# Counting split units anew in each stage of a hybrid decoder block

## The chip, the cores and the metric

The kernel runs on one core of a Trainium2 chip. The metric is the device time of one execution in microseconds (us), given as the median of several runs. An execution can also be recorded by the hardware profiler; the profile then shows the work of each engine: TensorE (PE, with its weight loads as PEld), VectorE (DVE), ScalarE (ACT), GpSimd (POOL) and SyncE (SP), which issues most of the DMA transfers here.

## The reference

One layer of a decoder block on 256 tokens of width 2048, in float32:

```
x = x + 0.5 * ffn1(rms_norm(x))                 # SwiGLU, hidden width 5632
z = rms_norm(x) @ w_in                          # 2048 -> 5120, five parts of 1024
y_lru = rg_lru(conv4(z0)) * gelu(z1)            # recurrent half
y_sc  = z2 * conv3(z3 * z4)                     # short convolution half
x = x + concat(rms_norm(y_lru), rms_norm(y_sc)) @ w_out
x = x + 0.5 * ffn2(rms_norm(x))
out = rms_norm(x)

ffn(h) = (silu(h @ w_gate) * (h @ w_up)) @ w_down
```

All matrix products are asked for in float32. The profile shows 339.82 MB read from HBM, nearly all of it weights, each used once for 256 rows.

## The kernel before

**Units and split parts.** Weights are worked off in *units* of 512 x 512 values, a tile of 128 x 2048 float32 (1 MB). `load` (L181) fetches a unit into one of three buffers of the pool `raws`. TensorE multiplies in a reduced float32 form, so each unit is split into two tiles of that form: `hi`, a rounded copy made by ScalarE in two halves, and `lo`, what is left (`raw - hi`), made by VectorE (`parts_of`, L210, and `low_part`, L204). A usual unit then takes 24 matmuls (the column products of the mixer are arranged otherwise): for each of two 128-row halves of the tokens, eight with `hi` and four with `lo`. In parts of the work seven products instead of eight are formed from a 2 x 2 arrangement of units (`seven`, L413); there a unit that belongs to the seven products takes 12 matmuls, and VectorE also forms sums and differences of raw units. Of those, two raw units are held longer and have buffers of their own (tag `kept`).

**Split buffers.** `split_tiles` (L194) hands out the pair of tiles for `hi` and `lo`. The pool `splits` lives for the whole kernel and has two such pairs, used in turn. While the list `extra` holds a pool, every third unit goes to that pool instead, in which there is one pair (where `extra[0]` is `bigs`, the pair comes from that general pool, which also lives for the whole kernel). `turn_of["split"]` counts the units; it is raised only while `extra` is not empty, and it is never set back.

**Stages.** They follow each other in this order. The first feed-forward part, `ffn(1, ...)` (L523), opens the pool `ffn1` and puts it into `extra`. The mixer opens two pools for the small tiles of the recurrent and the convolution halves; its column products take their split tiles from `splits` alone, and only `sc_c` (L1141) puts `bigs` into `extra`, for one call of `seven`. Still inside the mixer, the first quarter of the columns of `w_out` is multiplied (units named `o0_...`), with `extra` empty. Then the pool `outs` (L1253) is opened and put into `extra`: the last quarter of the columns (`o3_...`, four units) and a call of `seven` for the two middle ones (`o_q`, eleven units). Then `ffn(2, ...)` opens its pool `ffn2`. The pools of the mixer, of `outs` and of `ffn2` are opened one after the other on the same stack of memory, so a tile in a later pool can lie where tiles of the earlier one were, and its first writer waits until the earlier pool is out of use.

**Names in the profile.** Tiles are named after what they belong to, with numbers left out: `hi_g` and `hi_u` are the first units of gate and up weights of a feed-forward part, `hi_o` those of `o0` and `o3`, `hi_o_q_p` and `hi_o_q_x` those of `o_q` (`p` for the seven products, `x` for the others). In `outs`, `own` (L1294) and `done` (L1290) add results to the residual `xres` by VectorE; the last of these adds reads a saved product, `s_o_q`, which lies in the pool `outs`.

**The start of the second feed-forward part.** Its loop (L771) takes units in the order gate 0, up 0, gate 1, up 1, gate 2, up 2, gate 3, up 3, each with `unit` and `joint`, and between them calls the functions listed in `follow` (L633): the transposes of the residual's second quarter, the norm factor `r` and its row of factors (`pb`, `bc`), then the scaled and transposed quarters 2 and 3 (`xn`, `pt`, `units`), which are the other operand of gate 2, up 2, gate 3 and up 3. Of the adds into the residual, those for its third quarter come last.

**Order.** SyncE's transfers, TensorE's opening and the whole of the first feed-forward part's opening are held in the order of the program text. Elsewhere the framework plans the order of the instructions on each engine, from program order and from what its plan takes to be ready; on the chip each engine then works in that order, with semaphore waits that the framework sets.

Of the kernel before, what the change touches and what calls it, by code (L numbers as in the profile page):

```python
# [49 lines left out]
def hybrid_block(ctx: ExitStack, tc: tile.TileContext, a: dict, out: bass.AP):  # L50
# [13 lines left out]
    def flush():  # L64
        while pending:
            pending.popleft()[1]()
# [12 lines left out]
    bigs = ctx.enter_context(tc.tile_pool(name="bigs", bufs=10, side="left"))  # L79
# [5 lines left out]
    def bank(name):  # L85
        return psum.tile([P, 512], F32, tag="ps", name=name)
# [85 lines left out]
    def big(name):  # L172

        return bigs.tile([P, UK, 2 * S], F32R, tag="big", name=name)
# [2 lines left out]

    extra = []
    turn_of = {"split": 0}

    def load(src, name, pieces=((0, UK),), loaded=None, kept=False):  # L181
        if kept and extra[0] is not bigs:
            raw = extra[0].tile([P, UK, CW], F32, tag="kept", name=f"raw_{name}", bufs=2)
        elif kept:
            raw = bigs.tile([P, UK, CW], F32, tag="big", name=f"raw_{name}")
        else:
            raw = raws.tile([P, UK, CW], F32, tag="raw", name=f"raw_{name}")
        for i, e in pieces:
            sp.dma_start(raw[:, i:e, :], src[i * P : e * P].rearrange("(j p) c -> p j c", p=P))
            if loaded:  # L190
                loaded(i)
        return raw
# [185 lines left out]
    def seven_of(sf, x0, x1, v, spare, parts, meanwhile=None):  # L378

        a11, a12, a21, a22 = v[0, 0], v[0, 1], v[1, 0], v[1, 1]
        parts = dict(zip((4, 5, 6, 2), parts))
        quads = {4: spare, 5: a11, 6: a21, 2: a12}
        sf.update({0: stationary(x0, 0), 1: stationary(x1, 0), 3: stationary(x1, 1)})

        def high(i):
            hi, lo = parts[i]
            act.copy(hi, quads[i])
            sf[i] = [(hi[:, j, :], lo[:, j, :]) for j in range(UK)]  # L390

        def low(i):
            hi, lo = parts[i]
            dve.tensor_tensor(lo, quads[i], f32(hi), op=ALU.subtract)

        def two():
            dve.tensor_tensor(a21, a11, a21, op=ALU.subtract)
            dve.tensor_tensor(a11, spare, a11, op=ALU.subtract)

        def last():  # L400
            dve.tensor_tensor(a12, a12, a11, op=ALU.subtract)

        dve.tensor_tensor(spare, a21, a22, op=ALU.add)
        high(4)
        if meanwhile:
            meanwhile()
        low(4)
        return two, last, high, low

    def quad(tile):  # L410
        return tile.rearrange("p (j c) -> p j c", j=UK)
# [110 lines left out]

    def ffn(tag, norm, after, opening=False):  # L523
        with tc.tile_pool(name=f"ffn{tag}", bufs=1, side="left") as fp:
            extra.append(fp)
            wg, wu, wd = (a[f"ffn{tag}_w_{s}"][0] for s in ("gate", "up", "down"))

            def keep(name, dt=F32):
# [426 lines left out]
    def to_mixer(c, t):  # L955
# [4 lines left out]
        else:  # L960
            held["nm"].later(c)

    ffn(1, n1, to_mixer, True)
    nm = held["nm"]

# [3 lines left out]
    with tc.tile_pool(name="mixer", bufs=1, side="left") as mp, tc.tile_pool(name="mixw", bufs=2, side="left") as mw:  # L969
# [15 lines left out]
        def tmp(tag, name, w=S, dt=F32, bufs=2):  # L985
            return mw.tile([P, w], dt, tag=tag, name=f"{tag}_{name}", bufs=bufs)
# [154 lines left out]
        def sc_c(between):  # L1141
            r2 = work.tile([P, NT], F32, tag="r2", name="r2")
            dve.tensor_tensor(r2, nm.r, nm.r, op=ALU.mult)
            rt = [r2[:, t : t + 1] for t in range(NT)]
            room = [tmp(tag, "snap", 4 * S, bufs=1) for tag in "vd"]
            free = [b[:, o : o + CW] for b in room for o in (0, CW)]
            z = {}

            def turn(n):
                for f in range(0, 4, 2):  # L1150
                    pt = bank(f"pt_c{n}_{f}")
                    for i in range(2):
                        for t in range(NT):
                            o = i * S + t * P
                            pe.transpose(pt[:, o : o + P], z[t, n][:, (f + i) * P : (f + i + 1) * P], ident)
                    for i in range(2):
                        q = 4 * (1 - n) + f + i
                        c = tmp("cc", q, S + 2, bufs=8)
                        nc.gpsimd.memset(c[:, :2], 0.0)
                        act.copy(c[:, 2:], pt[:, i * S : (i + 1) * S])  # L1160
                        cc[q] = c

            def done(t, n, ps, tiles):
                for p in tiles[1:]:
                    dve.tensor_tensor(tiles[0], tiles[0], p, op=ALU.add)
                    free.append(p)
                if tiles:
                    z[t, n] = tiles[0]
                    dve.scalar_tensor_tensor(z[t, n], ps, rt[t], z[t, n], op0=ALU.mult, op1=ALU.add)
                else:  # L1170
                    z[t, n] = free.pop()
                    act.activation(z[t, n], ps, AF.Copy, scale=rt[t])
                if (t, n) == (1, 0):
                    turn(1)

            c0 = 3 * (D // 2)
            extra.append(bigs)
            seven(
                w_in, (0, 1), (c0 + CW, c0), si, [(u, nm.xT[u]) for u in (2, 3)], "in_c", lambda name: free.pop(0), done,
                lambda i: between() if i == 1 else None,  # L1180
                factor={"s1": rt[0], "s5": rt[1], "u2": rt[0], "u3": rt[1]},
            )
            extra.clear()
            return lambda: turn(0)
# [27 lines left out]
        for i, (use, part, half) in enumerate(order):  # L1212
            ps = columns(w_in, part * (D // 2) + half * CW, nm.xT, f"in_{part}_{half}", behind)
            behind = None
            if i == 0:
                flush()
                nm.factor()
                nm.diagonals()
                nm.rows()
                bc = nm.bc  # L1220
                behind = sc_c(lambda: use(ps, half))
                gate_weights("a", a["lru_w_a"][0])
                gate_weights("i", a["lru_w_i"][0])
                yT += [big(f"yT_{u}") for u in range(KD // UK)]
            else:
                use(ps, half)
# [6 lines left out]
        def add(c, t, g, *parts):  # L1233
            xr = xres[:, t, c * CW : (c + 1) * CW]
            for p in parts:
                dve.scalar_tensor_tensor(xr, p, rs[g][:, t : t + 1], xr, op0=ALU.mult, op1=ALU.add)
# [14 lines left out]


    with tc.tile_pool(name="outs", bufs=1, side="left") as op:  # L1253
        extra.append(op)

        def snapshot(name):
            return op.tile([P, CW], F32, tag="snap", name=name, bufs=4)

        so = {}
        pair = [big(f"ys_{i}") for i in range(2)]  # L1260
        halves_of = [(b[:, :, o : o + P], b[:, :, o + P : o + S]) for b in pair for o in (0, S)]
        quads = {(t, u): yv[0][:, :, u * S + t * P : u * S + (t + 1) * P] for t in range(NT) for u in range(2)}
        spare = quad(op.tile([P, CW], F32, name="yspare"))
        two, last_sum, high, low = seven_of(so, yT[0], yT[1], quads, spare, halves_of)

        def part(i):
            high(i)
            low(i)

        steps = {  # L1270
            (0, 0): [two, lambda: part(5)], (0, 1): [lambda: part(6)],
            (1, 0): [last_sum, lambda: part(2)], (1, 1): [],
        }
        for g in range(2):
            ps = product(
                w_out, 3, (2 * g, 2 * g + 1), yT.__getitem__, f"o3_{g}",
                between=lambda i: [fn() for fn in steps[g, i]],
            )
            for t in range(NT):
                add(3, t, g, ps[t])  # L1280
        n2.later(3, False)
        flush()
        left = {1: 4, 2: 4}

        def added(c):
            left[c] -= 1
            if not left[c]:
                n2.later(c, c < 2)

        def done(t, n, ps, tiles):  # L1290
            add(2 - n, t, 0, *([] if ps is None else [ps]), *tiles)
            added(2 - n)

        def own(t, n, ps):  # L1294
            add(2 - n, t, 1, ps)
            added(2 - n)

        seven(
            w_out, (0, 1), (2 * CW, CW), so, [(u, yT[u]) for u in (2, 3)], "o_q", snapshot, done, own=own
        )  # L1300
        extra.clear()
# [34 lines left out]
    def close(t, y3, h, n):  # L1336
# [24 lines left out]
        for engine, begin, end in ((dve, 0, 256), (dve, 256, 896), (act, 896, 1536), (dve, 1536, 2048)):  # L1361
# [6 lines left out]
            nc.sync.dma_start(ov[:, t, o], xo)  # L1368

    ffn(2, n2, last)  # L1370


# [28 lines left out]
```

## Time and profile before

| | |
|---|---|
| median of 3 runs | 1736.88 us (1736.38 to 1737.58) |
| profiled execution, its own time | 1733.94 us |
| its span, first to last instruction | 1732.2 us |
| PE busy | 1716.9 us (99%) |
| PEld busy | 1434.8 us (83%) |
| DVE busy | 1510.4 us (87%) |
| ACT busy | 1076.7 us (62%) |
| moved by DMA | 343.22 MB, mean 198 GB/s |
| mean granted TensorE clock | 0.997 |

Times in the profile are microseconds from the first instruction. The span is shorter than the execution's own time by what lies before the first and after the last instruction, and the profiled execution need not be the median one. "Idle" before an instruction is the time for which its engine did nothing, and the name behind the arrow is what ended it. A busy PE is not one at its peak, since matmuls are pipelined and their ends are modelled; an idle PE is idle.

### The profile page before, as it was taken

What the parts mean: (1) busy time and instruction counts of PE and PEld (TensorE: products, weight loads), DVE (VectorE), ACT (ScalarE), POOL (GpSimd) and SP (SyncE); (2) the same over time, 40 slices, a digit from 0 to 9 for tenths busy, and PEclk for the clock granted to TensorE, in tenths of its full rate; (3) what the DMA queues carried; (4) which work ended last, traced back from release to release, by engine and by line L of the source; (5) the groups of instructions that cost most, each with busy time, mean ns of one, the idle gap of its engine ahead of it and who ended that gap; (6) DMA issues with size and microseconds to landing.
All of it is one profiled execution on the core that took longest, in us unless ns stands there. A gap on an engine that the chain in (4) does not pass through costs nothing.

```text
span 1732.2 us, 20321 instructions
## 1 busy us (share of the span) xinstructions
PE 1716.9 (99%) x7985; PEld 1434.8 (83%) x7985; DVE 1510.4 (87%) x1239; ACT 1076.7 (62%) x1406; POOL 7.0 (0%) x34
## 2 busy tenths in 40 slices
PE   9999999999999999999999989999999999999998
PEld 8888888888888888888888878888888888888886
DVE  7998999899789887887897878889899887899895
ACT  7766566656566666666866556666556664556664
POOL 0100000000000000000000000000000000000000
PEclk9999999999999999999999999999999999999999
DMA  8564665666465646555566463575665646555743
GB/s 300 191 244 143 209 228 189 201 217 229 164 215 196 210 172 216 179 180 185 170 195 218 171 233 132 194 243 191 200 210 188 228 149 219 194 195 194 252 161 122
DMA packets 174223, 343.22 MB, mean 198 GB/s; under 512 B 5684, under 2 KB 8624, under 8 KB 174000
## 3 DMA queue, kind: packets, MB, share of 16 engines
q1 hardware_dynamic: 173632, 340.81, 58.1%
q8 instruction: 62, 1.02, 0.2%
q10 hardware_dynamic: 176, 1.06, 0.1%
q14 instruction: 33, 0.27, 0.0%
q0 software_dynamic: 320, 0.07, 0.0%
HBM read 339.82 MB, written 2.10 MB: 197 GB/s over the span
## 4 chain that ended last, share of the span: by engine, by line
PE 99%; DVE 0%; ACT 0%; issue 0%; DVEq 0%; ACTq 0%
PE ps_d L43 14%; PE ps_in L43 10%; PE ps_g_a L43 9%; PE ps_u_a L43 9%; PE ps_u_c L43 6%; PE ps_g_c L43 6%; PE ps_d_a L43 5%; PE ps_u_d L43 5%; PE ps_g_d L43 5%; PE ps_d_c L43 3%; PE ps_u_e L43 3%; PE ps_g_e L43 3%; PE ps_g L43 3%; PE ps_o L43 3%; PE ps_u L43 3%; PE ps_d_d L43 3%
## 5 line engine op out<-in xcount | busy, mean ns | idle before, releaser
L43 ACT CAST hi_g_p<-raw_g 128x1024 fp32r<-128x1024 f32 (+1 forms) x139 | 142.1, 1056 | 110.5 <-DVE raw_g L43 39.0
L43 DVE TENSOR_TENSOR lo_g_p<-raw_g,hi_g_p 128x2048 fp32r<-128x2048 f32 x70 | 159.6, 2287 | 32.8 <-ACT hi_g_p L43 32.7
L43 ACT CAST hi_u_p<-raw_u 128x1024 fp32r<-128x1024 f32 x140 | 141.4, 1050 | 66.2 <-PE ps_u_a L43 26.7
L43 DVE TENSOR_TENSOR lo_u_p<-raw_u,hi_u_p 128x2048 fp32r<-128x2048 f32 x70 | 159.2, 2287 | 15.1 <-ACT hi_u_p L43 14.8
L43 PE MATMUL ps_d<-hi_d,h 128*128 128x512 f32 x696 | 166.1, 390 | 0.0
L43 PEld LDWEIGHTS ps_d<-hi_d,h 128*128 128x128 f32 x696 | 130.0, 188 | 26.6
L43 ACT CAST hi_d<-raw_d 128x1024 fp32r<-128x1024 f32 x88 | 88.5, 1048 | 67.7 <-PE ps_u_d L43 19.9
L43 DVE TENSOR_TENSOR lo_d<-raw_d,hi_d 128x2048 fp32r<-128x2048 f32 x44 | 100.7, 2290 | 33.4 <-ACT hi_d L43 33.4
L43 PE MATMUL ps_in<-xT_nm,hi_in 128*128 128x512 f32 x512 | 122.5, 391 | 0.0
L43 ACT CAST hi_d_p<-raw_d 128x1024 fp32r<-128x1024 f32 x84 | 85.1, 1049 | 57.5 <-DVE raw_d L43 34.9
L43 PEld LDWEIGHTS ps_in<-xT_nm,hi_in 128*128 128x128 f32 x512 | 94.1, 188 | 18.9 <-ACT tha L43 0.5
L43 ACT CAST hi_u_x<-raw_u 128x1024 fp32r<-128x1024 f32 x80 | 80.6, 1047 | 38.7 <-PE ps_u_c L43 23.9
L43 ACT CAST hi_g_x<-raw_g 128x1024 fp32r<-128x1024 f32 (+1 forms) x79 | 81.3, 1059 | 32.4 <-PE ps_g_c L43 22.6
L43 DVE TENSOR_TENSOR raw_u<-raw_u,raw_u 128x2048 f32<-128x2048 f32 x40 | 91.6, 2290 | 10.7 <-DMA raw_u<-in_ffn_w_up_dram 10.0
L43 DVE TENSOR_TENSOR lo_d_p<-raw_d,hi_d_p 128x2048 fp32r<-128x2048 f32 x42 | 95.6, 2287 | 5.0 <-ACT hi_d_p L43 4.9
L43 DVE TENSOR_TENSOR lo_g_x<-raw_g,hi_g_x 128x2048 fp32r<-128x2048 f32 x40 | 91.5, 2287 | 8.4 <-ACT hi_g_x L43 8.4
L43 DVE TENSOR_TENSOR lo_in<-raw_in,hi_in 128x2048 fp32r<-128x2048 f32 x32 | 73.3, 2289 | 26.3 <-ACT hi_in L43 25.9
L43 DVE TENSOR_TENSOR raw_g<-raw_g,raw_g 128x2048 f32<-128x2048 f32 x40 | 91.5, 2288 | 5.0 <-DMA raw_g<-in_ffn_w_gate_dram 4.5
L43 DVE TENSOR_TENSOR lo_u_x<-raw_u,hi_u_x 128x2048 fp32r<-128x2048 f32 x40 | 91.4, 2286 | 0.8 <-ACT hi_u_x L43 0.4
L43 PE MATMUL ps_d<-lo_d,h 128*128 128x512 f32 x348 | 86.2, 389 | 0.0
L43 ACT CAST hi_in<-raw_in 128x1024 fp32r<-128x1024 f32 x64 | 64.0, 1046 | 24.9 <-PE ps_in L43 15.3
L43 PEld LDWEIGHTS ps_d<-lo_d,h 128*128 128x128 f32 x348 | 65.3, 188 | 13.6
(471 smaller groups left out, 3741.2 us busy)
## 6 DMA issues: line engine op xcount, KB each, us to landing
raw_d<-in_ffn_w_down_dram SPq DMA_DIRECT2D x88, 1024.0 KB, 5.2
raw_u<-in_ffn_w_up_dram SPq DMA_DIRECT2D x87, 1024.0 KB, 5.2
raw_g<-in_ffn_w_gate_dram SPq DMA_DIRECT2D x86, 1024.0 KB, 5.3
raw_in<-in_w_in_dram SPq DMA_DIRECT2D x32, 1024.0 KB, 5.1
raw_in_c<-in_w_in_dram SPq DMA_DIRECT2D x8, 1024.0 KB, 5.3
raw_o<-in_w_out_dram SPq DMA_DIRECT2D x8, 1024.0 KB, 5.1
raw_o_q<-in_w_out_dram SPq DMA_DIRECT2D x8, 1024.0 KB, 5.2
xres<-in_x_dram SPq DMA_DIRECT2D x3, 512.0 KB, 9.5
```

What stands on the lines that cost most here:

```text
L43: ins = getattr(self.engine, name)(*args, **kwargs)
```

## The change

A helper `more_from` puts a pool into `extra` and sets the count of split units back to zero. The three places that put a pool into `extra` call it.

```diff
     extra = []
     turn_of = {"split": 0}
+
+    def more_from(pool):
+        extra.append(pool)
+        turn_of["split"] = 0
...
     def ffn(tag, norm, after, opening=False):
         with tc.tile_pool(name=f"ffn{tag}", bufs=1, side="left") as fp:
-            extra.append(fp)
+            more_from(fp)
...
             c0 = 3 * (D // 2)
-            extra.append(bigs)
+            more_from(bigs)
             seven(
...
     with tc.tile_pool(name="outs", bufs=1, side="left") as op:
-        extra.append(op)
+        more_from(op)
```

So in each stage that has a pool in `extra`, the first and the second unit take their split tiles from `splits`, the third from the stage's pool, and so on. No instruction is added or removed by the text; which tiles are used, and with them the waits and the planned order, can differ.

## The prediction

> **What bounds the kernel now.** I read the page first, then the waits of TensorE, then the chain of work around the place where they lie.
>
> ```profile
> span 1732.2 us, 20321 instructions
> PE 1716.9 (99%) x7985; PEld 1434.8 (83%) x7985; DVE 1510.4 (87%) x1239; ACT 1076.7 (62%) x1406; POOL 7.0 (0%) x34
> PE 99%; DVE 0%; ACT 0%; issue 0%; DVEq 0%; ACTq 0%
> raw_g<-in_ffn_w_gate_dram SPq DMA_DIRECT2D x86, 1024.0 KB, 5.3
> ```
>
> TensorE is on the chain that ended last for 99% of the span. The change touches no matmul, so only TensorE's idle time, 1732.2 - 1716.9 = 15.3 us, can be won. Its waits are two rows:
>
> ```profile
> PE ps_g L43 <- ACT hi_g L43: 6.0, 2, 5.6
> PE idle L43 <- DVE ones L43: 1.1, 1, 1.1
> ```
>
> So one wait of 5.6 us stands out, on a `hi` tile of a gate unit; the second row is the kernel's start. The chain of waits from 900 to 1160 us, columns start and length, places it:
>
> ```profile
> 1024.06 0.68 DVE xres L43
> ...
> 1024.75 1.05 ACT hi_g L43
> ...
> 1025.85 7.24 PE ps_g L43 x24
> ...
> 1039.44 0.45 PE pb_n L43 x4
> 1039.89 5.46 PE ps_g L43 x24
> ...
> 1052.57 5.46 PE ps_g L43 x24
> ```
>
> It is the seam between `outs` and the second feed-forward part. Around it, in order of time (start, length, engine, instruction, and in brackets the idle time before it):
>
> ```profile
> 1009.23 1.98 PE L43 MATMUL ps_o_q_a<-hi_o_q_p,yT 128*128 128x512 f32 x8
> 1011.04 1.07 PE L43 MATMUL ps_o_q_a<-lo_o_q_p,yT 128*128 128x512 f32 x4
> ...
> 1015.77 2.00 ACT L43 CAST hi_u<-raw_u 128x1024 fp32r<-128x1024 f32 x2 [4.19 <-PE ps_o_q_x L43]
> 1016.68 0.75 DVE L43 SCALAR_TENSOR_TENSOR xres<-ps_o_q_x,r_y,xres 128x512 f32<-128x512 f32 x1 [4.41 <-PE ps_o_q_x L43]
> ...
> 1018.26 2.28 DVE L43 TENSOR_TENSOR lo_u<-raw_u,hi_u 128x2048 fp32r<-128x2048 f32 x1
> ...
> 1019.20 1.07 PE L43 MATMUL ps_o_q_d<-lo_o_q_p,yT 128*128 128x512 f32 x4
> 1019.40 2.00 ACT L43 CAST hi_g<-raw_g 128x1024 fp32r<-128x1024 f32 x2 [1.63 <-PE ps_o_q_d L43]
> 1020.46 0.74 DVE L43 SCALAR_TENSOR_TENSOR xres<-ps_o_q_a,r_y,xres 128x512 f32<-128x512 f32 x1
> ...
> 1021.77 2.28 DVE L43 TENSOR_TENSOR lo_g<-raw_g,hi_g 128x2048 fp32r<-128x2048 f32 x1
> 1023.97 0.75 DVE L43 SCALAR_TENSOR_TENSOR xres<-s_o_q,r_y,xres 128x512 f32<-128x512 f32 x1
> ...
> 1024.75 1.99 ACT L43 CAST hi_g<-raw_g 128x1024 fp32r<-128x1024 f32 x2 [3.36 <-DVE xres L43]
> ```
>
> Read it with the count. The first feed-forward part splits 8 opening units, ten calls of `seven` at 11, and in `down` 3 + 3 + 9, 4 + 4 + 11 and again 19: 8 + 110 + 53 = 171. `sc_c` adds 11, `outs` 4 + 11. So `outs` opens after 182 and the second feed-forward part after 197. Unit 198, gate 0, is a multiple of three and goes to the new pool; up 0 and gate 1 go to `splits`. The rows agree: up 0's copy waits for matmuls to leave a shared pair, gate 1's likewise (`ps_o_q_d`), and the copy that comes last, 1024.75, is gate 0's, released by the add that reads `s_o_q`, the last use of the pool `outs`. TensorE had ended at 1019.20 + 1.07 = 1020.27 and began again at 1025.85: **5.58 us** idle. The gate 0 group then took 7.24 us where its like at 1052.57 took 5.46. The windows say why (columns: stretch, length, busy time of PE, PEld, DVE, ACT, POOL, granted clock, DMA share, GB/s):
>
> ```profile
> 1012.00:1020.00 8.00, 8.00 (x37) 6.52 (x35) 3.44 (x4) 2.60 (x3) 0.00 (x0) 1.00 0.62 222
> 1020.00:1026.00 6.00, 0.42 (x3) 0.15 (x1) 5.97 (x7) 2.64 (x4) 0.00 (x0) 0.69 0.71 187
> 1026.00:1028.00 2.00, 2.00 (x5) 1.61 (x6) 1.27 (x2) 1.97 (x5) 0.00 (x0) 0.50 0.99 370
> 1028.00:1030.00 2.00, 2.00 (x8) 1.54 (x8) 1.63 (x5) 0.33 (x3) 0.00 (x0) 0.73 1.05 405
> 1030.00:1034.00 4.00, 4.00 (x23) 3.43 (x22) 1.15 (x5) 3.60 (x6) 0.00 (x0) 1.00 1.04 384
> ```
>
> The granted clock fell to half and came back within the group: 7.24 - 5.46 = **1.78 us** more.
>
> **The change part by part.** In the first feed-forward part nothing moves, since it starts at zero as before. In `sc_c` neither: 171 is a multiple of three, so its residues are the same. In the middle of a stage the count is only a name: three pairs go round, and every unit takes over the pair of the unit three before it, whatever the residue. What differs is where a stage begins.
>
> *Gate 0.* With `outs` counted from zero, its last units are numbered 13, 14 and 15: the third-last and second-last products' units lie in `splits`, the last in the pool. Gate 0 takes the pair of unit 13, which the rows 1009.23 and 1011.04 read: `hi` is free at 1011.21, `lo` at 1012.11. Its raw tile, as it is loaded now, has landed by then:
>
> ```profile
> 1003.05 0.37 SPq L43 DMA_DIRECT2D raw_g<-in_ffn_w_gate_dram  x1
> ...
> 1020.57 0.37 SPq L43 DMA_DIRECT2D raw_u<-in_ffn_w_up_dram  x1
> ...
> 1030.20 0.16 DVE L43 SCALAR_TENSOR_TENSOR r_n<-q_n,y_n 128x2 f32<-128x2 f32 x1
> ...
> 1046.32 1.65 DVE L43 SCALAR_TENSOR_TENSOR x<-pt_n,cols_many,x 128x256 fp32r<-128x256 f32 x4
> ```
>
> 1003.05 + 5.3 = 1008.4. So the copies (1.99) fit into ACT's idle 4.19 us before 1015.77, ending near 1013.6, and the low part (2.28) into DVE's idle 4.41 us before 1016.68, ending near 1015.9. Both are done 4 us before TensorE is free at 1020.27. The cover is the `outs` matmuls; without it the copy would cost up to its own 1.05 us for the first half. Gate 0's group then starts at 1020.27 with a clock that has not dropped: 5.58 + 1.78 = 7.36 us less.
>
> *Up 0* keeps its pair and its time. Its raw buffer goes on as before; gate 0's is given back at 1015.9, so the load now issued at 1020.57 can go out earlier, and those behind it on SP's queue are not later.
>
> *Gate 1* now gets the pool's pair and so the wait for `outs`. DVE no longer has gate 1's low part (1021.77) between the last adds: they follow up 0's low part, which ends at 1020.54, at 0.66 us each, and end near 1022.5. Copies 2.00 and low part 2.28 end near 1026.8; TensorE wants gate 1 at 1039.89 - 7.36 = 1032.5. Behind the waiting copy on ACT stand the squares of the last quarter and the rest of the norm, which need the same adds anyway. No cost.
>
> *The norm chain.* From the end of the last add to `r_n` it is 1030.36 - 1024.72 = 5.64 us now, with one low part in it; later there is again one, gate 1's. So `r_n` comes near 1028.1, and `pb_n` is wanted at 1039.44 - 7.36 = 1032.1.
>
> *The entry of `outs`.* There unit 183, `o3`'s first, has a fresh pair now, and the third would have it then. The first waits for a pair of `splits` instead:
>
> ```profile
> 945.14 3.92 PE L43 MATMUL ps_o<-hi_o,yT 128*128 128x512 f32 x16
> 948.90 1.98 PE L43 MATMUL ps_o<-lo_o,yT 128*128 128x512 f32 x8
> ...
> 956.52 3.92 PE L43 MATMUL ps_o<-hi_o,yT 128*128 128x512 f32 x16
> ...
> 960.43 1.41 DVE L43 SCALAR_TENSOR_TENSOR xres<-ps_o,r_y,xres 128x512 f32<-128x512 f32 x2
> 961.87 1.02 PEld L43 LDWEIGHTS pt_n<-ident,xres 128*128 128x128 f32 x8
> ```
>
> Its copies can begin at 949 (the `hi` matmuls from 945.14 are through) and end at 951, its low part can begin at 950.9 and end near 953.3; TensorE wants them at 956.52 and about 960. Nothing is lost unless DVE's order shifts so that the adds at 960.43 come one low part later: the transposes at 961.87 follow them by 0.03 us. So this part costs from 0 to 2.28 us; no gain is possible, as TensorE has no wait there. I take 0, since just as many low parts stand ahead of those adds as now. At the kernel's end the pairs again go round by three; I take 0.
>
> The sum is made against the profiled execution: 1733.94 - 7.36 = 1726.58 us. The median of the runs stands 1736.88 - 1733.94 = 2.94 us above it, so in the measure of the median the forecast is **1729.5 us**, 0.42% less.
>
> **The rivals.**
>
> *A, VectorE takes the place of the wait.* For it speaks that DVE was busy for 5.97 of 6 us during the stall, and that TensorE's order has seven more groups that each need DVE's parts. If the transposed third quarter (`x`, 1046.32, ends 1047.97) comes no earlier than now, TensorE, which would reach gate 2 at 1052.57 - 7.36 = 1045.21, waits 2.76 us: 1732.3. Against it: the chain ahead of it starts 2.2 us earlier, as worked out, so it would end near 1045.8 even with all gaps kept, 0.6 us late, and a gap of 2.77 us before the low part at 1033.65 is there to be closed:
>
> ```profile
> 1033.65 2.29 DVE L43 TENSOR_TENSOR lo_u<-raw_u,hi_u 128x2048 fp32r<-128x2048 f32 x1 [2.77 <-ACT hi_u L43]
> ```
>
> [...]
>
> *B, the entry of `outs` loses a low part's time.* 7.36 - 2.28 = 5.08 us remain: 1731.8. For it speaks the 0.03 us of slack; against it that DVE's work there is the same in amount.
>
> *C, the change does not do what it says*, or the wait moves whole to gate 1 or the norm chain: if my count were off by one, gate 0 would not have been on the pool. 1736.9. Against it stands that its copy is the one released by `xres`.
>
> *D, slower: low parts crowd the norm chain.* The plan may put the low parts of gate 1, up 1 and gate 2 all ahead of the third quarter's transposed tile on DVE. Three more at 2.28 move its end from 1047.97 to 1054.8; TensorE, due at 1045.21, waits 9.6 us and loses 1.78 to the clock: 11.4 - 7.36 = 4.0 us slower, 1740.9. It decides against the change from an end of about 1050.8 on, 2.8 us later than now (a wait of 5.6 with its 1.78). Against it: each of these low parts needs a copy that itself waits for matmuls to leave a pair, so they can't all be ready early.
>
> **How the numbers follow.** Forecast 0.64, A 0.17, B 0.07, C 0.07, D 0.05. From no change this measurement tells about 0.2%, 3.5 us, so faster means below 1733.4 us. The forecast and B lie there, and of A most (0.13; with the clock's loss, or a somewhat longer wait, 0.04 falls within). So faster 0.84, same 0.04 + 0.07 = 0.11, slower 0.05. The range goes from 1728.0, since the order near the end may win or lose a microsecond or so, to 1734.0, which takes in A with its dearer end.
>
> **What would show it right or wrong.** Right: a copy of `hi_g` between 1011 and 1016 us; TensorE with no wait on `ps_g` at the seam, a first group of 5.5 us and a granted clock of 1.00 from 1020 to 1034; the third unit's copy released by `xres` near 1022.5; the entry of `outs` without a gap. Wrong: a PE wait on `x`, `pb_n` or `pt_n` between 1025 and 1060 (A, D), one near 960 (B), or `hi_g` still ending a long wait near 1025 (C). The forecast is wrong if TensorE's idle time falls by less than 3 us, whatever the cause.

## The result and the profile after

| | before | after |
|---|---|---|
| median of 6 runs each, us | 1736.66 (1734.26 to 1738.51) | 1727.14 (1726.79 to 1729.1) |
| profiled execution, us | 1733.94 | 1726.79 |
| its span, us | 1732.2 | 1725.0 |

The changed kernel takes 0.9947 of the time, interval [0.9934, 0.996]: 9.2 us less (6.9 to 11.5). The two profiled executions differ by 7.15 us, where 7.36 had been worked out, but the medians by 9.52. So there are two things to explain: a gain that came as forecast in the profile, and some 2 us more of it in the medians.

The page of the changed kernel, its span and first engine line, and then the waits of TensorE (what waited for what: us in total, times, longest):

```profile
span 1725.0 us, 20330 instructions
PE 1715.1 (99%) x7985; PEld 1432.9 (83%) x7985; DVE 1509.3 (87%) x1239; ACT 1077.6 (62%) x1406; POOL 7.0 (0%) x34
```

```profile
PE idle L43 <- DVE ones L43: 1.1, 1, 1.1
PE ps_g L43 <- ACT hi_g L43: 0.6, 1, 0.6
```

TensorE's idle time went from 15.3 to 9.9 us, which is 5.4 less; its busy time went down by another 1.8, the slowed first group. The wait of 5.6 us is gone. What is left on `ps_g` is the kernel's start. The chain of waits of the changed kernel from 1010 to 1045 us (start, length):

```profile
1017.60 2.72 PE ps_o_q_d L43 x12
1020.32 5.44 PE ps_g L43 x24
1025.77 0.87 PE pt_n L43 x8
1026.64 5.47 PE ps_u L43 x24
1032.11 3.40 PE ps_g L43 x15
1035.51 0.56 PE pb_n L43 x4
1036.07 2.08 PE ps_g L43 x9
```

Gate 0 follows the last product of `outs` without a gap and takes 5.44 us, not 7.24. Below, the same stretch of the changed kernel in order of time (in brackets the idle time of the engine before the instruction, and what ended it), and its windows (stretch, length, busy PE, PEld, DVE, ACT, POOL, granted clock, DMA share, GB/s):

```profile
1011.29 2.00 ACT L43 CAST hi_g<-raw_g 128x1024 fp32r<-128x1024 f32 x2 [0.24 <-PE ps_o_q_a L43]
...
1013.32 2.29 DVE L43 TENSOR_TENSOR lo_g<-raw_g,hi_g 128x2048 fp32r<-128x2048 f32 x1 [1.33 <-ACT hi_g L43]
...
1021.94 0.75 DVE L43 SCALAR_TENSOR_TENSOR xres<-s_o_q,r_y,xres 128x512 f32<-128x512 f32 x1
...
1023.42 1.03 ACT L43 CAST hi_g<-raw_g 128x1024 fp32r<-128x1024 f32 x1
...
1026.04 2.29 DVE L43 TENSOR_TENSOR lo_g<-raw_g,hi_g 128x2048 fp32r<-128x2048 f32 x1 [0.57 <-ACT hi_g L43]
...
1029.89 2.27 DVE L43 TENSOR_TENSOR lo_u<-raw_u,hi_u 128x2048 fp32r<-128x2048 f32 x1
...
1032.36 2.29 DVE L43 TENSOR_TENSOR lo_g<-raw_g,hi_g 128x2048 fp32r<-128x2048 f32 x1
...
1034.76 0.16 DVE L43 SCALAR_TENSOR_TENSOR r_n<-q_n,y_n 128x2 f32<-128x2 f32 x1
...
1035.39 0.68 PE L43 MATMUL pb_n<-diag_n,ones 128*128 128x128 f32 x4
...
1039.20 1.65 DVE L43 SCALAR_TENSOR_TENSOR x<-pt_n,cols_many,x 128x256 fp32r<-128x256 f32 x4
...
1045.12 3.21 PE L43 MATMUL ps_g<-hi_g,x 128*128 128x512 f32 x13
```

```profile
1020.00:1026.00 6.00, 6.00 (x30) 4.97 (x29) 4.28 (x8) 3.21 (x7) 0.00 (x0) 1.00 0.72 239
1026.00:1028.00 2.00, 2.00 (x13) 1.74 (x12) 1.96 (x1) 2.00 (x7) 0.00 (x0) 1.00 1.01 379
```

Gate 0's copy is now released by TensorE (`ps_o_q_a` gives its pair back), 13.5 us earlier than before. The copy that follows the last add is now gate 1's, and its low part ends at 1028.33, 3.8 us before TensorE wants the unit. The granted clock stays at 1.00.

The reader should also see what did *not* go as forecast. `r_n` comes at 1034.76, not near 1028.1: the low parts of gate 1, up 1 and gate 2 all stand ahead of it on VectorE. TensorE does not wait all the same, because the planned order has moved as well: `pb_n`, a group of its own before, now sits between the 15th and the 16th matmul of gate 1, and the third quarter's `x` ends at 1040.85, 7.1 us earlier than before, well ahead of gate 2 at 1045.12.

### The profile page after: what moved, and what is told of

The parts are those of the page before. It is cut to its first block, busy times and chain, and to the rows that moved or that the text cites. A ratio compares the mean times of both kernels' runs of the same rounds, so it can differ in the third digit from the quotient of the medians.

```text
span 1725.0 us, 20330 instructions
## 1 busy us (share of the span) xinstructions
PE 1715.1 (99%) x7985; PEld 1432.9 (83%) x7985; DVE 1509.3 (87%) x1239; ACT 1077.6 (62%) x1406; POOL 7.0 (0%) x34
## 4 chain that ended last, share of the span: by engine, by line
PE 99%; DVE 0%; ACT 0%; DVEq 0%; issue 0%; ACTq 0%
PE ps_d L43 14%; PE ps_in L43 10%; PE ps_g_a L43 9%; PE ps_u_a L43 9%; PE ps_u_c L43 6%; PE ps_g_c L43 6%; PE ps_d_a L43 5%; PE ps_u_d L43 5%; PE ps_g_d L43 5%; PE ps_d_c L43 3%; PE ps_u_e L43 3%; PE ps_g_e L43 3%; PE ps_g L43 3%; PE ps_o L43 3%; PE ps_u L43 3%; PE ps_d_d L43 3%
## 5 line engine op out<-in xcount | busy, mean ns | idle before, releaser
L43 ACT CAST hi_in<-raw_in 128x1024 fp32r<-128x1024 f32 x64 | 64.0, 1045 | 24.9 <-PE ps_in L43 15.4
```

Source lines behind the costliest of these rows:

```text
L43: ins = getattr(self.engine, name)(*args, **kwargs)
```

## The experiments

Each kernel was run on one chip with runs of the kernel before beside it; ratios are to those, with their 95% intervals. The kernel before had medians of 1736.2 us (27 runs), 1736.38 (21) and 1737.08 (15) in the three groups. The first two sections below ask how large the loss at the seam really is.

### The kernel before once more

No edit.

> The kernel before, unchanged, for the time and clock of each of its runs. Theory 1 (the seam explains all): the profile recorded so far, 1733.94 us, is a cheap execution; the wait at the seam is about 5.6 us in every run, but the half clock after it lasts longer in most, so runs go from 1734 to 1738.5 us and the slower ones show a lower mean granted clock (0.997 in the cheap one). Theory 2 (the excess of some 2.7 us over the profiled execution lies elsewhere, at the start or in the transfers): mean clocks stay equal at 0.997 while times differ.

Measured: 1736.78 us (1735.78 to 1737.94), ratio 1.0003 [0.9995, 1.0012]; its profiled execution took 1736.78 us, 2.84 more than the one the prediction was made from. Its chain, its windows and its waits of TensorE at the same places:

```profile
1025.78 8.57 PE ps_g L43 x24
```

```profile
1020.00:1026.00 6.00, 0.42 (x2) 0.22 (x2) 5.94 (x7) 2.64 (x4) 0.00 (x0) 0.91 0.66 201
1026.00:1028.00 2.00, 2.00 (x5) 1.62 (x6) 1.29 (x1) 1.97 (x5) 0.00 (x0) 0.50 1.02 393
1028.00:1030.00 2.00, 2.00 (x6) 1.55 (x5) 1.63 (x6) 0.26 (x2) 0.00 (x0) 0.50 1.05 399
1030.00:1034.00 4.00, 4.00 (x15) 3.19 (x15) 0.74 (x4) 2.80 (x4) 0.00 (x0) 0.78 1.05 385
```

```profile
PE ps_g L43 <- ACT hi_g L43: 6.2, 2, 5.6
PE ps_d_a L43 <- DVE lo_d_p L43: 1.5, 1, 1.5
```

The wait has the same 5.6 us, but the clock dropped later in it (0.91 over 1020 to 1026 instead of 0.69), so more of the slow stretch fell on matmuls, and the first group took 8.57 us instead of 7.24. And there is a second wait, of 1.5 us, which the earlier profile did not have. 1.33 + 1.46 = 2.79 us, nearly all of the 2.84. So neither of the two theories holds alone: a part of the excess is the clock's and a part lies in a transfer. The mean clocks of the 11 runs, 0.996 or 0.997, do not follow their times. The second wait has its root 23 us earlier (timeline of this kernel, all on VectorE but the last row):

```profile
1653.31 0.43 DVE L43 TENSOR_SCALAR fin<-fin 128x512 f32<-128x512 f32 x1 [2.89 <-DMA fin<-in_final_norm_dram]
...
1671.79 2.28 DVE L43 TENSOR_TENSOR lo_d_x<-raw_d,hi_d_x 128x2048 fp32r<-128x2048 f32 x1
...
1674.60 6.69 DVE L43 TENSOR_TENSOR lo_d_p<-raw_d,hi_d_p 128x2048 fp32r<-128x2048 f32 x3
...
1676.93 1.20 PE L43 MATMUL ps_d_a<-lo_d_p,hs 128*128 128x512 f32 x4 [1.46 <-DVE lo_d_p L43]
```

VectorE stands still for 2.89 us until the final norm's gains (`fin`) have landed, 7.3 us after they were issued; in the profile of the prediction they landed after 5.6 and the same wait was 1.22. VectorE is behind from there on, and the low part that TensorE needs next is queued after `lo_d_x`. The five profiles with this order go together: `fin` is waited for 1.22 us in that of the prediction and 1.2 in fill_half below, and TensorE does not wait; 2.0 in fill_three_quarters, and it waits 0.5; 2.8 in fill_seam, and it waits 1.3; 2.89 here, and it waits 1.46. In the changed kernel the same instruction waits nearly as long, but VectorE's planned order is another one:

```profile
1644.45 0.43 DVE L43 TENSOR_SCALAR fin<-fin 128x512 f32<-128x512 f32 x1 [2.49 <-DMA fin<-in_final_norm_dram]
...
1664.14 2.28 DVE L43 TENSOR_TENSOR lo_d_p<-raw_d,hi_d_p 128x2048 fp32r<-128x2048 f32 x1
...
1666.35 2.28 DVE L43 TENSOR_TENSOR lo_d_x<-raw_d,hi_d_x 128x2048 fp32r<-128x2048 f32 x1
...
1666.48 1.20 PE L43 MATMUL ps_d_a<-lo_d_p,hs 128*128 128x512 f32 x4
```

Here `lo_d_p` comes before `lo_d_x`, and TensorE does not wait. The prediction did not foresee this order; that it hides the late transfer is luck of the plan.

### Keeping TensorE busy at the seam

```diff
             else:
+                pe.held = True
+                for _ in range(24):
+                    pe.matmul(ps["g", 0][:, :P], ones, ones, start=True, stop=True)
+                pe.held = False
                 for u in range(KD // UK):
```

The kernel before, with products of ones (each recorded as two matmuls) held ahead of gate 0; gate 0's own group overwrites what they write. With 24 they cover the wait, with 12 and 18 a part of it.

> The kernel before with 24 small matmuls of ones on TensorE between the last product of the outs stage and gate 0 of the second feed-forward part, into a bank that gate 0 overwrites; they fill about 5.3 us of the 5.58 us wait. The wait for gate 0's hi tile stays (gate 0 starts near 1025.9), the idle time does not. Theory 1: the clock stays at 1.00, the first group takes 5.46 instead of 7.24 us, the profiled span falls by 1.8 us to 1730.4, and the median falls by more, 4 us, to about 1732.5, with runs within 1.5 us of each other. Theory 2: the median falls by 1.8 us at most, to about 1735, and the runs spread as before.

> The same with 12 small matmuls, so that about 2.8 us of the wait are left idle. If a wait of this length does not drop the clock (rival A's cheaper end): first group of gate 0 5.46 us, the same time as with 24. If it does: granted clock of 0.5 for part of the first group and about 7.2 us for it, the same time as the kernel before.

> The kernel before with 18 small matmuls in the wait at the seam, so that about 1.4 us of it stay idle (2.9 us with 12, where the clock fell in the profiled run). If the clock falls only when a wait reaches some length between these: first group 5.5 us, mean clock 0.998 to 0.999 in all runs, median as with 24, 1734.1 us. If any wait can bring it down: some runs at 0.996 or 0.997 and a median nearer to 1736.

| kernel | fillers | median, us | ratio | wait left, us | first group, us |
|---|---|---|---|---|---|
| fill_seam | 24 | 1734.13 | 0.9985 [0.9976, 0.9994] | 0.21 | 5.72 |
| fill_three_quarters | 18 | 1734.66 | 0.9985 [0.9976, 0.9994] | 1.55 | 5.72 |
| fill_half | 12 | 1736.06 | 0.9998 [0.9989, 1.0007] | 2.89 | 7.11 |

Of the timelines of TensorE, first the kernel with 24 fillers, then the one with 18, then the one with 12:

```profile
1020.37 5.52 PE L43 MATMUL ps_g<-ones 128*128 128x128 f32 x48
1026.11 3.90 PE L43 MATMUL ps_g<-hi_g,xT_n 128*128 128x512 f32 x16 [0.21 <-ACT hi_g L43]
```

```profile
1027.49 3.90 PE L43 MATMUL ps_g<-hi_g,xT_n 128*128 128x512 f32 x16 [1.55 <-ACT hi_g L43]
```

```profile
1026.79 5.30 PE L43 MATMUL ps_g<-hi_g,xT_n 128*128 128x512 f32 x16 [2.89 <-ACT hi_g L43]
```

And the windows of the kernel with 12:

```profile
1023.00:1027.00 4.00, 1.11 (x10) 0.92 (x9) 3.95 (x4) 1.31 (x2) 0.00 (x0) 0.92 0.90 281
1027.00:1030.00 3.00, 3.00 (x8) 2.41 (x9) 2.29 (x2) 2.03 (x5) 0.00 (x0) 0.54 1.01 391
```

With the clock kept up and the wait still there in time, the kernel gains 2.6 us (1.0 to 4.2), between the two theories. Its first group is 0.28 us longer than the changed kernel's 5.44, so the clock's part is 2.6 + 0.28, about 2.9 us. This is the cost of the clock alone, averaged over runs; the prediction had 1.78, which this interval by itself does not rule out. (The profiled span of fill_seam, 1732.3 us, did not fall to the 1730.4 expected: it has the late `fin` and a wait of 1.3 us on `ps_d_a`.) A remaining wait of 1.55 us loses nothing of it that shows: the clock held in the profile (1.00 from 1020 to 1034), and all 11 runs had a mean granted clock of 0.998 or 0.999, as with 24 fillers. A remaining wait of 2.89 us dropped the clock in the profiled execution (0.54 from 1027 to 1030). The runs differ in it: 6 of the 11 had a mean clock of 0.996 or 0.997, which no run with 18 or 24 fillers had, and two had 0.999, as if it had not dropped; the other three had 0.998, like the profiled one, and do not tell.

Why the same wait costs 1.78 us in one execution and 3.11 in another can be read from windows of 0.1 us in the four profiles where the clock fell:

| profile | TensorE idle from | clock falls to 0.5 | after idle, us | back at 1.00 | first group begins | longer by, us |
|---|---|---|---|---|---|---|
| before | 1020.27 | 1022.3 | 2.0 | 1029.1 | 1025.85 | 1.78 |
| before_again | 1020.20 | 1025.0 | 4.8 | 1031.8 | 1025.78 | 3.11 |
| no_fin_op (below) | 1021.50 | 1026.1 | 4.6 | 1032.9 | 1027.08 | 3.01 |
| fill_half | 1023.90 | 1026.3 | 2.4 | 1029.8 | 1026.79 | 1.39, against 5.72 |

After each of the three full waits the clock stayed at half for 6.8 us, after the short one for 3.4. What differs is how far into the wait it fell, and so how much of the slow stretch was left for matmuls: 3.2, 6.0, 5.8 and 3.0 us, of which half, 1.6, 3.0, 2.9 and 1.5 us, is close to the time lost.

### Without the scaling of the final gains

```diff
-            if t == 0:
-                lastgain = fin[:, D - CW :]
-                dve.tensor_scalar(lastgain, lastgain, -0.5, None, op0=ALU.mult)
...
-        dve.tensor_tensor(y3[:, h * w : (h + 1) * w], xres[:, t, o], fin[:, o], op=ALU.mult)
+        dve.scalar_tensor_tensor(y3[:, h * w : (h + 1) * w], xres[:, t, o], -0.5, fin[:, o], op0=ALU.mult, op1=ALU.mult)
```

The factor moves into the last products, so VectorE no longer stops for `fin`. It was done to the kernel before (no_fin_op), to that with 24 fillers (fill_no_fin_op), and to the changed kernel (after_no_fin_op).

> The kernel before without the one VectorE operation that scales the last quarter of the final norm's gains (0.43 us); its factor -0.5 goes into the multiplication that uses them, so the result is the same. That operation waits for the gains' transfer, 1.2 us in the profile before but 2.9 us in the second profile of the same kernel, where TensorE then waits 1.5 us for a low part (ps_d_a). Theory (the transfer's late landing is the second part of the excess): no TensorE wait on ps_d_a, median 0.7 to 1.0 us lower, 1735.4, and the slowest runs nearer to 1737.5 than to 1738.8. Rival (only the clock's phase makes the excess): no difference beyond 0.3 us.

> Both at once on the kernel before: 24 small matmuls in the wait at the seam, and no gains operation. What is left against the changed kernel is then the wait of 5.58 us itself and 0.3 us of the filler. Theory: 1727.2 + 5.9 = 1733.1 us, with runs within 2 us of each other. Rival (there is a third source of the excess): 1734.1 as with the filler alone.

> The changed kernel without the gains operation. Its profile shows the operation waiting 2.5 us and TensorE waiting nowhere after it, so the theory is the same time as the changed kernel, 1727.1 within 0.5 us; if the spread of the changed kernel (1726.8 to 1729.1) comes from this transfer, the slow runs go and the median falls by up to 0.4 us.

| kernel | median, us | ratio |
|---|---|---|
| no_fin_op | 1736.05 (1733.72 to 1737.68) | 0.9996 [0.9988, 1.0005] |
| fill_no_fin_op | 1733.34 (1732.62 to 1734.56) | 0.9983 [0.9975, 0.9992] |
| after_no_fin_op | 1728.69 (1726.47 to 1729.63) | 0.9952 [0.9938, 0.9966] |

In the profiles of the first two the wait on `ps_d_a` is gone, as it should be. In the times this can't be told from nothing: 0.0002 between fill_seam and fill_no_fin_op is 0.3 us, 0.0004 for no_fin_op alone 0.7 us, and both lie inside their intervals. (The profile of no_fin_op had its own first group at 8.47 us and a wait of 1.1 us at the kernel's start, so one execution would mislead here.) For the changed kernel the edit brings nothing that shows (its median lies 1.6 us above the 1727.1 expected; its profile waits 1.5 us for `xres` at the kernel's start), which agrees with the profile after, where that stop has no follower. So the second wait is real in single executions, up to 1.5 us, and worth 0.3 to 0.7 us by these ratios, without proof that it is more than zero; the interval of no_fin_op reaches to 2 us.

### Which of the three resets matters, and which unit

In the first kernel the reset stands in `ffn` alone, so `sc_c` and `outs` count on as before; in the second the second feed-forward part starts at one, so that its second unit, up 0, falls on the new pool.

```diff
             extra.append(fp)
+            turn_of["split"] = 0
```

> The kernel before with the count set to zero in the feed-forward parts alone; outs is entered as before, and gate 0 takes the pair of the second-last unit of outs (hi free near 1015.8, lo near 1017.6), up 0 that of the last. Theory: only gate 0 on the new pool made the wait, so this gives the whole gain, within 0.5 us of the changed kernel, 1727.1 us. Rival: the entry of outs has a part in it; then 1 us or more of the gain is missing.

```diff
             extra.append(fp)
+            turn_of["split"] = 0 if tag == 1 else 1
```

> The kernel before with the count set to one at the start of the second feed-forward part, so that its second unit, up 0, takes the new pool's pair, and gate 0 one of splits. Theory: up 0's copy waits for the last add that reads the outs pool, near 1022.5, its first half is there at 1023.6 and its low part near 1027; TensorE wants it at 1026.6 and 1030.2, so no wait and the same 1727.1 us within 0.5. Rival: the low part crowds the norm chain on VectorE and TensorE waits 1 to 3 us, 1728 to 1730.

Measured: reset_ffn_only 1727.46 us (1727.32 to 1729.67), ratio 0.9952 [0.9938, 0.9965], no wait at the seam, first group 5.44. From the start of gate 0 to the end its profile takes 704.7 us, as that of the changed kernel does. The one reset does the whole of it, and the one in `outs` is neither needed nor, within the interval, harmful. second_on_pool 1729.34 us (1727.89 to 1730.13), ratio 0.9959 [0.9947, 0.9972]: no wait of TensorE at the seam either, because the planned order puts groups of gate 1 between pieces of up 0 and so wants up 0's second half and its low part later. The median is 2 us above the 1727.1 expected, and in the range of the rival, but the rival's wait is not there: from gate 0 to the end the profile takes 705.0 us, 0.4 more than the changed kernel's, and gate 0 begins only at 1022.46. The intervals overlap those of the changed kernel; a loss of a microsecond or so is possible, not shown.

### The changed kernel once more, and with more work on VectorE

The first is without an edit. The second forms the low part twice for gate 1, up 1 and gate 2, which adds 3 x 2.28 = 6.8 us to VectorE inside the norm chain: rival D's mechanism, laid on by hand.

> The changed kernel once more, for more runs of it. [...] Theory: a median of 1727.1 to 1728.3 us, none above 1730, and a mean clock of 0.998 to 0.999 in all runs.

```diff
-        low_part(raw, hi, lo)
+        for _ in range(2 if name in ("g2_0_1", "u2_0_1", "g2_0_2") else 1):
+            low_part(raw, hi, lo)
```

> The changed kernel in which VectorE computes the low parts of gate 1, up 1 and gate 2 of the second feed-forward part twice, the second time with the same result: 3 x 2.29 = 6.9 us more work on VectorE right where rival D put it. In the changed kernel's profile the third quarter's transposed operand is complete at 1040.9 and TensorE takes it at 1045.1. If VectorE has the 4.3 us to spare but no more: TensorE waits up to 2.6 us before gate 2, and the time is up to 2.6 us above the changed kernel. If the planned order moves the work aside: no wait, the same time. If it is as tight as rival D had it: 6.9 us and the clock's loss, 1736.

Measured: after_again 1727.82 us (1727.11 to 1729.28), ratio 0.995 [0.9937, 0.9962]; more_low_parts 1727.84 us (1727.41 to 1729.44), ratio 0.9949 [0.9937, 0.9962]. The extra 6.8 us cost nothing that the medians show; in the profile the stretch from gate 0 to the end is 1.3 us longer than in that of the changed kernel (706.0 and 704.7 us). Its timeline:

```profile
1038.04 0.15 DVE L43 SCALAR_TENSOR_TENSOR r_n<-q_n,y_n 128x2 f32<-128x2 f32 x1
...
1040.84 0.61 PE L43 MATMUL pb_n<-diag_n,ones 128*128 128x128 f32 x4
1041.29 0.82 PE L43 MATMUL pt_n<-ident,xn 128*128 128x128 f32 x6
...
1054.43 2.11 PE L43 MATMUL ps_g<-lo_g,x 128*128 128x512 f32 x8 [0.29 <-DVE lo_g L43]
```

`r_n` comes another 3.3 us later (1.4 of them because gate 0 itself begins later, at 1021.74), and the plan puts `pb_n` and pieces of `pt_n` among up 1's matmuls, where there is other work to do. The only wait that follows in this stretch is 0.29 us.

The profiled execution of after_again took 1729.28 us, 2.49 more than that of the changed kernel's first profile, with the same instructions and a first group of 5.44 in both. It reaches gate 0 at 1023.06 instead of 1020.32, so its difference lies ahead of the seam; from gate 0 to the end it takes 704.4 us against 704.7. Most of it, 1.8 us, has built up by 14 us, beginning in the kernel's first matmuls (first the profile after, then after_again); the rest is mainly the wait in the last line below, 0.8 us near 101 us, in the first feed-forward part:

```profile
5.64 1.21 PE L43 MATMUL ps_g<-hi_g,xT_n 128*128 128x512 f32 x4 [0.63 <-ACT hi_g L43]
```

```profile
5.88 2.08 PE L43 MATMUL ps_g<-hi_g,xT_n 128*128 128x512 f32 x4 [0.22 <-ACT hi_g L43]
```

```profile
PE ps_u_c L43 <- DVE lo_u_p L43: 0.8, 1, 0.8
```

## Why the prediction was right in place, and wrong in its sum

**The wait and its place: right.** 5.58 us at gate 0 and a drop of the clock behind it, both gone when gate 0 takes a pair that earlier matmuls give back. reset_ffn_only shows that the reset at the second feed-forward part alone brings it, second_on_pool that another start which keeps gate 0 off the new pool takes the wait away too, and fill_seam that the two parts of the loss are separate.

**Gate 0, up 0, gate 1: right in place and cost.** Gate 0's copy ran from 1011.29 to 1013.29 (1011.21 to near 1013.6 forecast), its low part to 1015.61 (near 1015.9), and the last add ended at 1022.69 (near 1022.5). Gate 1's low part was 1.5 us later than forecast, since squares of the norm were taken between the halves of its copy; there were 3.8 us to spare.

**The norm chain: no cost, as forecast, but by luck.** "The norm chain ... later there is again one" low part: there were three, and `r_n` came 6.7 us later than forecast. This is the crowding of rival D, but not its 11.4 us: D took TensorE's order as fixed, while the plan put `pb_n` and the third quarter elsewhere. So the prediction's reason for no cost failed, and the moved order, which it did not foresee, made up for it. more_low_parts shows how much room there is: 6.8 us more work costs 1.3 us in its profile and nothing in the medians. Rival A fell for the same reason.

**The entry of outs: no cost, in part by luck.** The order did shift: the adds at 960.43 came at 962.06, the kind of shift on which the prediction had put a loss. But TensorE found other work; the transposes are planned in pieces among `o3`'s second unit (TensorE's timeline of the changed kernel):

```profile
962.12 1.30 PE L43 MATMUL ps_o<-hi_o,yT 128*128 128x512 f32 x5
963.26 0.60 PE L43 MATMUL pt_n<-ident,xres 128*128 128x128 f32 x4
963.61 0.48 PE L43 MATMUL ps_o<-hi_o,yT 128*128 128x512 f32 x1
```

So rival B did not come about, and C fell with the first row of the timeline after the change.

**A row that was read too coarsely.** The clock of 0.69 over 1020 to 1026 already says that it stood at half for some 3.7 of these 6 us, so it fell 2.0 us after TensorE stopped. An early fall made the loss look small, and the sum took 1.78 us for a fixed price. For rival A's wait of 2.76 us the range and the chances took the clock's loss as possible (the "dearer end"); no run shows that term of 1.78 us after such a wait. In its place fill_half, with 2.89 us left, lost 1.39 us in its profile (7.11 against 5.72), and fill_three_quarters, with 1.55 us left, none (5.72).

**The step that failed: the clock's term, and with it the way from the profiled execution to the median.** "The median of the runs stands 1736.88 - 1733.94 = 2.94 us above it": that offset was carried over to the changed kernel as if it had nothing to do with the change. In the runs it went from 2.72 us (1736.66 - 1733.94) to 0.35 (1727.14 - 1726.79). The second of these is in part chance, as the offset of one execution is: the changed kernel's other profile stands 1.46 us above its median. The profile of before was a cheap execution: at 1733.94 us it is shorter than each of the 80 timed runs of that kernel (6 with the result, 63 beside the experiments, 11 of before_again). What made it cheap are in part the very things that the change takes away:

- the clock's loss, 1.78 us in the sum, was 3.11 in before_again (8.57 - 5.46), 3.01 in no_fin_op, and about 2.9 on average by fill_seam: roughly 1.1 us were missing;
- a late `fin` and the wait behind it, zero in the sum, 1.46 us in before_again, and not exposed in the changed kernel's order: 0.3 to 0.7 us by the ratios, not told from zero.

With these, 5.58 + 2.9 + 0 to 0.7 gives 8.5 to 9.2 us. The runs gave 9.2 (6.9 to 11.5), and after_again 8.7 (6.6 to 10.9). The first ratio's interval holds the forecast's own 0.9958 too, at its upper end, so by this ratio alone the excess is not certain. Pooled over the groups, the means of the 80 runs of the kernel before and of the 11 of the changed one differ by 8.8 us, give or take 0.6 by their scatter, which leaves 7.36 out. Which two terms vary is in the profiles. The lower end of the range, 1728.0, allowed 1.5 us for "the order near the end" and nothing for a term that was read at its low end; that is why it was too high. What the runs do not settle is how the excess divides between the two terms: each average carries an interval of some 1.5 us either way.

No kernel tried is better than the changed one: after_no_fin_op and reset_ffn_only lie within its interval.

## What to carry to other kernels

When buffers go round by a count across stages, ask for each stage which unit is the first writer of a pool that lies on old memory, and give that place to one that TensorE wants late. The stall here had two terms in its price, its length (5.58 us) and the clock's slow time behind it (1.78, 3.01 and 3.11 us in three profiles); the second varied with how far into the wait the clock fell (2.0, 4.6 and 4.8 us), so take it as a range, and compare the profiled execution with all the timed runs before carrying its offset to the median over: terms that vary and that the change removes are part of that offset. A late helper on VectorE cost little here (1.3 us in the profile of more_low_parts for 6.8 us more work) because TensorE's planned order had other groups to put ahead of it.

## What the runs showed of the hardware

- **A wait of under 3 us can drop the clock.** With 2.89 us left, the granted clock fell to 0.54 in the window behind it and the first group took 7.11 us; with 1.55 us left it held at 1.00 in the profile, and the mean clocks of its 11 runs, 0.998 or 0.999, are like those with 24 fillers. The falls came 2.0 us (the profile of before), 2.4 us (fill_half), 4.6 us (no_fin_op) and 4.8 us (before_again) after TensorE went idle. No single length decides it in these four profiles; the shortest idle time before a fall was 2.0 us. Two of the runs with 2.89 us left in the profile had a mean clock of 0.999, so at that length the fall seems not to come in every run.
- **The same wait does not cost the same.** After 5.6 us of idle time the slow stretch ended at 1029.1 in the profile of before and at 1031.8 in before_again, for a loss of 1.78 or 3.11 us. It lasted 6.8 us in both; in the first it began 2.8 us sooner after TensorE stopped.
- **The kernel's start scatters.** The same four matmuls took 1.21 and 2.08 us at 5.6 to 5.9 us from the start in two executions of the same kernel. The granted clock reads 1.00 in the windows of both from 0 to 12 us, so what slows them was not found.
- **A transfer's landing scatters by as much as a small stall.** `fin`, issued once, landed after 5.6 us in one execution and 7.3 in another of the same kernel.
